# A decoder layer's output projection: attention rows in one tile pair, loaded in token halves by ScalarE, and the attention half first

## The chip, the cores and the metric

The kernel runs on one core of one Trainium2 chip. A core has a matrix engine (TensorE, in the profile PE, with its weight loads as PEld), three engines for elementwise work (VectorE or DVE, ScalarE or ACT, GpSimd or POOL), a synchronisation engine (SyncE or SP) that here only issues transfers, and 16 DMA engines that move data between DRAM and the core's own memory (SBUF) behind queues that SP, ACT and POOL feed. Each engine runs its own list of instructions in order and waits on semaphores where an operand or a buffer is not ready. The metric is device microseconds for one execution, the median of several. Before the change it is 1192.65 us (three runs, 1191.54 to 1194.22).

## The reference

One layer of a hybrid decoder over 1024 prompt tokens and 64 decode tokens (8 sequences of 8), model width 1024. Two mixers read one input projection: retention (8 heads of 64) and sliding-window attention (8 heads of 64). Their two results of 512 columns each are laid side by side and go through one output projection:

```python
h = x + jnp.concatenate([o_r, o_s], axis=-1) @ w_out     # 1088 x 1024 times 1024 x 1024
hf = rms_norm(h, norm_ffn_gain)
h = h + jnp.square(jax.nn.relu(hf @ w_up)) @ w_down      # 1024 -> 4096 -> 1024
```

`o_r` is the normalised and gated retention result, `o_s` the attention result. The change touches the first of these lines, and the buffers that the last one inherits from it. All is float32.

## The kernel before

**Arithmetic.** Every float32 operand is split into a rounded high part and a low remainder, and a product is three matmuls: high by high, low by high, high by low (`mm3`, lines 171 to 174; the profile shows them as L172, L173, L174, and L174 is the one that reads the low part of the moving operand). A split is `halve` (line 786): ACT casts the high part (L787), DVE or POOL subtracts to get the low part (L788). So each weight tile costs one ACT cast and one DVE subtraction before its first three matmuls can all run.

**Stages.** Input projection; sliding-window attention, whose results go as high and low parts to DRAM (`ms_hi_d`, `ms_lo_d`); retention in blocks t = 0 to 7 of 128 tokens and a decode block 8; the output projection; a product-saving two-level scheme for the MLP's up projection (`up`), which writes its activations to DRAM (`u_d`), and for its down projection, which reads them back (`ur`, split into `uh` and `ul`) and accumulates in the tiles `a`. The 1088 tokens are two groups s = 0, 1 of 544, each two halves h of 272: one matmul has 272 columns.

**Output projection.** It is transposed: for each m of 8 blocks of 128 output columns and each h, a PSUM tile `pso` gathers four k-steps of the retention half (weights `wor_m`, data `mixrh`, `mixrl`) and four of the attention half (`woa_m`, `mixah`, `mixal`): 24 matmuls. `wo_pair` (line 815) loads the raw weights of two m in one transfer on SP's queue (names ending in `_raw`) and splits them. `mix_load` (line 808) fetches the attention results of one s from DRAM, as one transfer of 1088 KB for the high and one for the low part, issued by SP (L811). The retention results come out of `mix_block`, in which ACT writes `mixrh` (L778) and POOL `mixrl` (L779). `residual` (line 831) fetches the residual input `y` by POOL's queue (L833), adds, stores it, and scales it for the MLP.

For s = 0 the projection (`out_early`) is interleaved with retention blocks 5, 6 and 7, two values of m behind each block, and m = 6, 7 behind the decode block. Its first values m = 0, 1 have the halves in the order retention, attention at h = 0 and attention, retention at h = 1. For s = 1 it runs alone after retention (`out_parts`), first the attention half of m = 0, 1, then the retention half.

**Memory.** Pools on the right side are placed one behind the other from the upper end of memory. At its upper end stands, up to the last `value_block`, the normalised input; the pools `mw` (weights `wa`, raw weights), `o`, `mxA` (attention rows of s = 1) and `mx0` (those of s = 0) take its place when the matmuls of `value_block` have read it. These are the matmuls `pst`. Later the pool `w` holds four weight tiles with the tag `wb`; in the MLP, weight tiles go to `wa` and `wb` in turn.

**What sets the order.** The program is written in the order above, and a planner, which simulates the engines, then sets each engine's list. So an edit can move instructions far from the place where it stands. The list of an engine is fixed when the kernel runs: an engine that waits for one instruction lets none behind it pass.

Of the kernel before, what the change touches and what calls it, by code (L numbers as in the profile page):

```python
# [20 lines left out]
P = 128  # L21
# [3 lines left out]
Q = 272  # L25
# [11 lines left out]
def hymba_layer(ctx: ExitStack, tc: tile.TileContext, a: dict, o: dict):  # L37
# [752 lines left out]
    def wsplit(src, tag, name, lo_eng):  # L790
        w = (mid if tag == "wb" else mw).tile([P, 2, 512], F32R, tag=tag, name=name, bufs=4)
        halve(w[:, 0, :], w[:, 1, :], src, lo_eng)
        return w
# [12 lines left out]
    mix, acc, fs, last_out = {}, {}, {}, [None]  # L806

    def mix_load(s, pl):
        for x, d_ in zip("hl", (ms_hi_d, ms_lo_d)):
            t_ = mix[s, "a" + x] = pl.tile([P, 4, 2, Q], F32R, tag="mixa" + x, name=f"mixa{x}{s}")  # L810
            nc.sync.dma_start(  # L811
                t_.bitcast(F32).rearrange("p k h n -> p k (h n)"), d_[:, :, 2 * Q * s : 2 * Q * s + 2 * Q]
            )
# [11 lines left out]
    def out_half(s, half, ps, h, w, first, last):  # L825
        for k in range(4):
            lh, ll = (w[:, i, k * 128 : k * 128 + 128] for i in range(2))
            mh, ml = (mix[s, half + x][:, k, h, :] for x in "hl")
            last_out[0] = mm3(ps, lh, ll, mh, ml, first and k == 0, last and k == 3)

    def residual(s, m, pss):
        y = om.tile([P, 2, Q], F32, tag="y", name=f"y{s}_{m}", bufs=2)
# [23 lines left out]
    def out_parts(s, ms, half, psum, pss):  # L856

        for m in ms:
            if m % 2 == 0:
                gen = wo_pair(s, m, half)  # L860
            w = next(gen)
            for h in range(2):
                if half == "a":
                    pss[m, h] = psum()
                out_half(s, half, pss[m, h], h, w, half == "a", half == "r")
# [89 lines left out]
    proj.close()  # L955
    mw = ctx.enter_context(pool("mw", side="right"))
# [5 lines left out]
    mxA = ox.enter_context(pool("mxA", side="right"))  # L962
    mx0x = ExitStack()
    mx0 = mx0x.enter_context(pool("mx0", side="right"))
    early = lambda: psA.tile([P, 512], F32, tag="mm", name="pso")[:, :Q]

    def out_early(m):

        if m and m % 2 == 0:
            gens["a"], gens["r"] = (wo_pair(0, m, x) for x in "ar")  # L970
            ahead.extend(next(gens[x]) for x in "ar")
        wa_, wr_ = ahead
        ahead.clear()
        if m % 2 == 0:
            ahead.extend(next(gens[x]) for x in "ar")
        pss = [early() for h in range(2)]
        for h in range(2):
            parts = [("a", wa_), ("r", wr_)]
            if m < 2 and h == 0:
                parts.reverse()  # L980
            for n, (half, w) in enumerate(parts):
                out_half(0, half, pss[h], h, w, n == 0, n == 1)
        residual(0, m, pss)()

    gens = {x: wo_pair(0, 0, x) for x in "ra"}
    ahead = [next(gens[x]) for x in "ra"][::-1]
    mix_load(0, mx0)
# [3 lines left out]
    for t in (5, 6, 7):  # L991
        mt = retention_block(t)
        for m in (2 * t - 10, 2 * t - 9):
            out_early(m)
        if t == 6:
            with tc.issue_after(last_load[0].ins):
                mix_load(1, mxA)
        mix_block(t, *mt)
    mix_block(8, *mt8)
    for m in (6, 7):  # L1000
        out_early(m)
# [52 lines left out]
    out_parts(1, (0, 1), "a", late, pss)  # L1054
# [6 lines left out]
    for ms in ((0, 1), (2, 3), (4, 5), (6, 7)):  # L1061
        if ms[0]:
            out_parts(1, ms, "a", late, pss)
        out_parts(1, ms, "r", late, pss)
# [20 lines left out]
    mid = ctx.enter_context(pool("w", side="right"))  # L1085
    ux = ExitStack()
# [304 lines left out]
```

## Time and profile before

| what | value |
|---|---|
| median of three runs | 1192.65 us (1191.54 to 1194.22) |
| the profiled execution, its own time | 1190.13 us |
| its span | 1188.3 us |
| mean granted TensorE clock in it | 0.998 |
| PE busy | 1173.1 us, 99% |
| DVE, ACT, POOL busy | 838.7 us, 513.6 us, 488.6 us (71%, 43%, 41%) |
| output projection's matmuls, first to last | 374.6 to 497.5 us in the span |

The span runs from the first to the last instruction of the profiled execution, and its own time lies 1.8 us above it. That execution lies 2.5 us below the median of the timed ones, so differences are to be formed inside one execution and then set against its own time or against the median, not mixed. In the rows of a timeline the columns are the start, the duration, the engine, the line, the operation and its tiles; in square brackets stands the idle time of the engine before the row, and what it waited for. Ends of matmuls are modelled: each is shown with about 0.29 us, while matmuls of 272 columns that follow one another start 0.125 us apart.

### The profile page before, as it was taken

How to read it: one execution, taken by the hardware profiler on the slowest of the kernel's cores; microseconds unless marked ns; L12 is line 12 of the kernel's file. 1: busy time of each engine (PE TensorE's matmuls, PEld its weight loads, DVE VectorE, ACT ScalarE, POOL GpSimd, SP SyncE). 2: the span in 40 equal slices, each digit the busy share in tenths (PEclk: the TensorE clock that was granted, in tenths of full speed). 3: DMA queues.
4: the chain of work that ended last, by engine and by line, in shares of the span. 5: the costliest groups of instructions: out<-in, count | busy, mean ns of one | idle time of the engine just before them, and what ended most of it. 6: DMA issues, size and time to landing. Idle time of an engine off the chain costs nothing.

```text
span 1188.3 us, 23487 instructions
## 1 busy us (share of the span) xinstructions
PE 1173.1 (99%) x9405; PEld 1126.8 (95%) x9405; DVE 838.7 (71%) x1546; ACT 513.6 (43%) x1055; POOL 488.6 (41%) x393
## 2 busy tenths in 40 slices
PE   9999999999999999999999999999999999999998
PEld 8999988989777999999999999999899999999998
DVE  7556768632356969887766677676788787888676
ACT  8343544553233437644444444444652333333231
POOL 0135333332434532466666666566472142053000
PEclk9999999999999999999999999999999999999999
DMA  7211234333326654343444434444684456443215
GB/s 246 73 62 68 92 102 169 101 116 103 99 72 229 210 165 155 116 156 124 149 152 148 146 128 142 149 148 158 246 278 149 153 171 201 143 163 97 76 59 187
DMA packets 102276, 169.44 MB, mean 143 GB/s; under 512 B 11999, under 2 KB 68255, under 8 KB 101911
## 3 DMA queue, kind: packets, MB, share of 16 engines
q1 hardware_dynamic: 87751, 122.68, 30.7%
q10 hardware_dynamic: 11856, 36.34, 9.4%
q0 software_dynamic: 2560, 8.91, 2.4%
q8 instruction: 74, 1.21, 0.4%
q14 instruction: 35, 0.29, 0.1%
HBM read 114.30 MB, written 53.61 MB: 141 GB/s over the span
## 4 chain that ended last, share of the span: by engine, by line
PE 83%; DVE 7%; issue 3%; DMA 2%; POOL 2%; ACT 2%; SPq 0%; ACTq 0%; DVEq 0%; POOLq 0%
PE psd L173 9%; PE psd L172 9%; PE psd L174 9%; PE psx L172 5%; PE psx L174 5%; PE psx L173 5%; PE psz L172 2%; PE psz L174 2%; PE psz L173 2%; PE pst L172 2%; PE pst L173 2%; PE pst L174 2%; PE psf L172 2%; PE psf L174 2%; PE psf L173 2%
## 5 line engine op out<-in xcount | busy, mean ns | idle before, releaser
L172 PE MATMUL psd<-uh,wd_w 128*128 128x272 f32 x896 | 259.1, 289 | 3.4 <-ACT a L1256 2.3
L173 PE MATMUL psd<-uh,wd_w 128*128 128x272 f32 x896 | 260.0, 290 | 0.0
L174 PE MATMUL psd<-ul,wd_w 128*128 128x272 f32 x896 | 258.5, 289 | 0.0
L172 PEld LDWEIGHTS psd<-uh,wd_w 128*128 128x128 f32 x896 | 169.8, 190 | 4.5 <-ACT a L1256 3.0
L174 PEld LDWEIGHTS psd<-ul,wd_w 128*128 128x128 f32 x896 | 169.4, 189 | 0.0
L173 PEld LDWEIGHTS psd<-uh,wd_w 128*128 128x128 f32 x896 | 169.1, 189 | 0.0
L1259 DVE TENSOR_TENSOR a<-a,psd 128x272 f32<-128x272 f32 x248 | 101.9, 431 | 50.4 <-PE psd L174 50.2
L788 DVE TENSOR_TENSOR wu_w<-wu_s,wu_w 128x512 fp32r<-128x512 f32 x64 | 59.7, 937 | 50.4 <-ACT wu_w L787 49.7
L787 ACT CAST wd_w<-wd_s 128x512 fp32r<-128x512 f32 x64 | 37.4, 623 | 115.8 <-PE psd L174 104.0
L788 DVE TENSOR_TENSOR ul<-ur,uh 128x1088 fp32r<-128x1088 f32 x56 | 81.8, 1487 | 2.8 <-ACT uh L787 2.8
L1113 DVE SCALAR_TENSOR_TENSOR m<-m,rsf 128x272 f32<-128x272 f32 x96 | 74.6, 777 | 3.2 <-ACT rsf L910 0.5
L172 PE MATMUL psx<-op_1h,wu_w 128*128 128x272 f32 x256 | 74.3, 290 | 0.4 <-ACT m L1129 0.4
L174 PE MATMUL psx<-op_1l,wu_w 128*128 128x272 f32 x256 | 74.1, 289 | 0.0
L172 PE MATMUL psx<-op_0h,wu_w 128*128 128x272 f32 x256 | 74.1, 290 | 0.0
L174 PE MATMUL psx<-op_0l,wu_w 128*128 128x272 f32 x256 | 74.1, 289 | 0.0
L173 PE MATMUL psx<-op_1h,wu_w 128*128 128x272 f32 x256 | 73.7, 288 | 0.0
L173 PE MATMUL psx<-op_0h,wu_w 128*128 128x272 f32 x256 | 73.7, 288 | 0.0
L362 POOL TENSOR_TENSOR sp<-sp,ssp 128x1024 f32<-128x1024 f32 (+1 forms) x16 | 28.6, 1789 | 88.4 <-DVE ssp L361 60.0
L172 PE MATMUL psf<-hnh,wqk_hi 128*128 128x384 f32 (+1 forms) x192 | 63.5, 331 | 0.2 <-DVE qkst L514 0.2
L787 ACT CAST uh<-ur 128x1088 fp32r<-128x1088 f32 x56 | 59.6, 1101 | 9.5 <-PE psd L173 9.1
L174 PE MATMUL psf<-hnl,wqk_hi 128*128 128x384 f32 (+1 forms) x192 | 63.2, 329 | 0.0
L173 PE MATMUL psf<-hnh,wqk_lo 128*128 128x384 f32 (+1 forms) x192 | 62.8, 327 | 0.0
(342 smaller groups left out, 3618.7 us busy)
## 6 DMA issues: line engine op xcount, KB each, us to landing
ur<-u_d SPq DMA_DIRECT2D x51, 544.0 KB, 5.0
u_d<-r4t SPq DMA_DIRECT2D x32, 544.0 KB, 4.5
wu_r<-in_w_up ACTq DMA_DIRECT2D x32, 512.0 KB, 4.4
wd_r<-in_w_down ACTq DMA_DIRECT2D x30, 512.0 KB, 6.6
u_d<-r3t SPq DMA_DIRECT2D x32, 408.0 KB, 2.7
y<-in_xY POOLq DMA_DIRECT2D x16, 272.0 KB, 3.2
y_d<-y POOLq DMA_DIRECT2D x16, 272.0 KB, 2.9
yt<-y_d SPq DMA_DIRECT2D x16, 272.0 KB, 2.8
```

Of the source, the lines that this page charges most:

```text
L172: nc.tensor.matmul(ps, lh, rh, start=first, stop=False, skip_group_check=more)
L173: nc.tensor.matmul(ps, ll, rh, start=False, stop=False, skip_group_check=more)
L174: return nc.tensor.matmul(ps, lh, rl, start=False, stop=last, skip_group_check=more)
L362: nc.gpsimd.tensor_tensor(s, s, ss.unsqueeze(2).broadcast_to([P, 4, n]), ALU.mult)
L787: nc.scalar.copy(hi, src)
L788: lo_eng.tensor_tensor(lo, src, hi.bitcast(F32), ALU.subtract)
L1113: nc.vector.scalar_tensor_tensor(t_, src, 0.0, rsf[:, s, h, :], ALU.max, ALU.mult)
L1259: added[i] = nc.vector.tensor_tensor(to, to, ps, ALU.add).ins
```

## The change

The attention rows of both s lie in one tile pair in a pool of its own, `mxw`, opened first on the right side, that is at the upper end of memory. `mix_load` fills it in four transfers of 544 KB, token half by token half; for s = 0 ACT issues them, for s = 1 SP does after the last matmuls of s = 0. In every step of s = 0 the attention half comes first; m = 6 and 7 are done together, all attention parts and then all retention parts. For s = 1 the first values m = 0, 1 begin with the retention half. The `y` tiles of s = 0 have four buffers, in `mx0`. PSUM tiles of s = 0 beyond the third come from a second pool. When the output projection has ended, the attention tiles are reused as the four `wb` weight tiles.

```diff
     def wsplit(src, tag, name, lo_eng):
-        w = (mid if tag == "wb" else mw).tile([P, 2, 512], F32R, tag=tag, name=name, bufs=4)
+        if tag == "wb":
+            w = wbs[wbn[0] % 4]
+            wbn[0] += 1
+        else:
+            w = mw.tile([P, 2, 512], F32R, tag=tag, name=name, bufs=4)
         halve(w[:, 0, :], w[:, 1, :], src, lo_eng)
...
-    def mix_load(s, pl):
-        for x, d_ in zip("hl", (ms_hi_d, ms_lo_d)):
-            t_ = mix[s, "a" + x] = pl.tile([P, 4, 2, Q], F32R, tag="mixa" + x, name=f"mixa{x}{s}")
-            nc.sync.dma_start(
-                t_.bitcast(F32).rearrange("p k h n -> p k (h n)"), d_[:, :, 2 * Q * s : 2 * Q * s + 2 * Q]
-            )
+    def mix_load(s, eng):
+        for x in "hl":
+            mix[s, "a" + x] = mxw.tile([P, 4, 2, Q], F32R, tag="mixa" + x, name=f"mixa{x}{s}")
+        for h in range(2):
+            c0 = Q * (2 * s + h)
+            for x, d_ in zip("hl", (ms_hi_d, ms_lo_d)):
+                eng.dma_start(mix[s, "a" + x].bitcast(F32)[:, :, h, :], d_[:, :, c0 : c0 + Q])
...
-        y = om.tile([P, 2, Q], F32, tag="y", name=f"y{s}_{m}", bufs=2)
+        y = (om if s else mx0).tile([P, 2, Q], F32, tag="y", name=f"y{s}_{m}", bufs=2 if s else 4)
...
     proj.close()
+    mxw = ctx.enter_context(pool("mxw", side="right"))
     mw = ctx.enter_context(pool("mw", side="right"))
...
-    mxA = ox.enter_context(pool("mxA", side="right"))
...
-    early = lambda: psA.tile([P, 512], F32, tag="mm", name="pso")[:, :Q]
...
+    def early(n):
+        pl, tag, bufs = (psA, "mm", 3) if n < 3 else (psB, "t1", 2)
+        return pl.tile([P, 512], F32, tag=tag, name="pso", bufs=bufs)[:, :Q]
...
-        for h in range(2):
-            parts = [("a", wa_), ("r", wr_)]
-            if m < 2 and h == 0:
-                parts.reverse()
-            for n, (half, w) in enumerate(parts):
-                out_half(0, half, pss[h], h, w, n == 0, n == 1)
-        residual(0, m, pss)()
...
+        parts = [(m, h, x) for m in ms for h in range(2) for x in "ar"]
+        if len(ms) == 2:
+            parts.sort(key=lambda p_: p_[2])
+        for m, h, x in parts:
+            if x == "a":
+                pss[m, h] = early(len(pss))
+            out_half(0, x, pss[m, h], h, ws[m, x], x == "a", x == "r")
+        for m in ms:
+            residual(0, m, [pss[m, h] for h in range(2)])()
 
-    gens = {x: wo_pair(0, 0, x) for x in "ra"}
-    ahead = [next(gens[x]) for x in "ra"][::-1]
-    mix_load(0, mx0)
+    mix_load(0, nc.scalar)
+    gens = {x: wo_pair(0, 0, x) for x in "ar"}
+    ahead = [next(gens[x]) for x in "ar"]
...
-            out_early(m)
-        if t == 6:
-            with tc.issue_after(last_load[0].ins):
-                mix_load(1, mxA)
+            out_early((m,))
         mix_block(t, *mt)
     mix_block(8, *mt8)
-    for m in (6, 7):
-        out_early(m)
+    out_early((6, 7))
+    mix_load(1, nc.sync)
...
-    out_parts(1, (0, 1), "a", late, pss)
+    out_parts(1, (0, 1), "r", late, pss)
...
     for ms in ((0, 1), (2, 3), (4, 5), (6, 7)):
+        out_parts(1, ms, "a", late, pss)
         if ms[0]:
-            out_parts(1, ms, "a", late, pss)
-        out_parts(1, ms, "r", late, pss)
+            out_parts(1, ms, "r", late, pss)
...
     mid = ctx.enter_context(pool("w", side="right"))
+    for x in "hl":
+        t_ = mxw.tile([P, 4, 2, Q], F32R, tag="mixa" + x, name="wb" + x).rearrange("p k h n -> p (k h n)")
+        wbs.extend(t_[:, i : i + 1024].rearrange("p (j n) -> p j n", j=2) for i in (0, 1024))
```

The planner's lists change at the places below. In them `woa_0` is the attention half's weight tile for m = 0, `wor_0` the retention half's; `state` is the retention state that DVE updates with the PSUM tile `pur`; `orrr` the head norm of a retention block and `mtr` its normalised result, which PE then transposes into `pm`.

VectorE, where the output projection begins, behind the last product `rptr` of retention block 5, before:

```order
L713 TENSOR_TENSOR rptr_4115<-rsr_4108,intra 128x512
L788 TENSOR_TENSOR wor_0_4218<-wor_0_raw,wor_0_4218 128x512
L749 SCALAR_TENSOR_TENSOR state_3387<-state_3386,decs,pur_4027 64x64 x8
L612 TENSOR_REDUCE orrr_4047<-osqr_4045 128x8
L788 TENSOR_TENSOR woa_0_4223<-woa_0_raw,woa_0_4223 128x512
L788 TENSOR_TENSOR woa_1_4328<-woa_0_raw,woa_1_4328 128x512
L788 TENSOR_TENSOR wor_1_4331<-wor_0_raw,wor_1_4331 128x512
L613 TENSOR_SCALAR orrr_4047<-orrr_4047 128x8
L615 TENSOR_TENSOR mtr_4044<-ror_4004,orrr_4047 128x512
```

And with the change:

```order
L713 TENSOR_TENSOR rptr_4115<-rsr_4108,intra 128x512
L749 SCALAR_TENSOR_TENSOR state_3387<-state_3386,decs,pur_4027 64x64 x8
L612 TENSOR_REDUCE orrr_4047<-osqr_4045 128x8
L788 TENSOR_TENSOR woa_0_4224<-woa_0_raw,woa_0_4224 128x512
L613 TENSOR_SCALAR orrr_4047<-orrr_4047 128x8
L788 TENSOR_TENSOR wor_0_4229<-wor_0_raw,wor_0_4229 128x512
L788 TENSOR_TENSOR woa_1_4330<-woa_0_raw,woa_1_4330 128x512
L788 TENSOR_TENSOR wor_1_4333<-wor_0_raw,wor_1_4333 128x512
L615 TENSOR_TENSOR mtr_4044<-ror_4004,orrr_4047 128x512
```

The first low part that PE's list asks for stood ahead of the eight state updates (`wor_0`) and now stands behind them and behind the reduction of `orrr` (`woa_0`); the short `orrr` step L613 stands two subtractions earlier.

TensorE at the same place, first rows behind `pur`, before (twelve matmuls of `wor_0` stand first, and then four of `woa_0`):

```order
L737 MATMUL pur_4027<-vtr_3606,kdr_4002 64x64 x8
L172 MATMUL pso<-mixrh,wor_0_4218 128x272
L173 MATMUL pso<-mixrh,wor_0_4218 128x272
L174 MATMUL pso<-mixrl,wor_0_4218 128x272
L172 MATMUL pso<-mixrh,wor_0_4218 128x272
```

With the change (twelve of `woa_0`, and then twelve of `wor_0`):

```order
L737 MATMUL pur_4027<-vtr_3606,kdr_4002 64x64 x8
L172 MATMUL pso<-mixah_4216,woa_0_4224 128x272
L173 MATMUL pso<-mixah_4216,woa_0_4224 128x272
L174 MATMUL pso<-mixal_4217,woa_0_4224 128x272
L172 MATMUL pso<-mixah_4216,woa_0_4224 128x272
```

Before, 30 matmuls of `pso` stand between `pur` and the transposes `pm`; with the change 32 of them and two matmuls `rsr` of the next block's scores.

ScalarE, where the down projection begins (`ur` are activations read back from DRAM, `uh_74` their high parts, `wd_r` raw down weights that ACT's queue loads, `a` the accumulators that ACT copies from PSUM), before:

```order
L1114 ACTIVATE r_1_10070<-m_1_9917 128x272
L1214 DMA ur_74_10084<-u_d_131 128x4x272 x2
L1214 DMA ur_5_10087<-u_d_131 128x4x272
L1256 COPY a_10093<-psd 128x272 x8
L787 CAST wd_w_10242<-wd_s_10240 128x512
L787 CAST wd_w_10307<-rw_6_9947 128x512
L787 CAST wd_w_10369<-wd_s_10168 128x512
L787 CAST wd_w_10372<-wd_s_9952 128x512
L802 DMA wd_r_10586<-in_w_down 128x1024
L787 CAST uh_74_10085<-ur_74_10084 128x1088
L802 DMA wd_r_10588<-in_w_down 128x1024
L1256 COPY a_10178<-psd 128x272
```

And with the change (the lines of the changed kernel are numbered 12 higher here; `wbh` and `wbl` are the reused tiles):

```order
L787 CAST wbl<-rw_6_9905 128x512
L1126 ACTIVATE r_1_10027<-m_1_9876 128x272
L1226 DMA ur_74_10041<-u_d_131 128x4x272 x2
L1226 DMA ur_5_10044<-u_d_131 128x4x272
L1268 COPY a_10050<-psd 128x272 x8
L787 CAST wbl<-wd_s_10195 128x512
L787 CAST wd_w_10322<-wd_s_10124 128x512
L787 CAST wbh<-wd_s_9910 128x512
L806 DMA wd_r_10536<-in_w_down 128x1024
L806 DMA wd_r_10538<-in_w_down 128x1024
L787 CAST uh_74_10042<-ur_74_10041 128x1088
L1268 COPY a_10133<-psd 128x272
```

The cast of `uh_74` stood ahead of the second `wd_r` transfer and now stands behind it, between it and the copy `a`; the cast of `rw_6` moved ahead of `r_1`.

More of the change, by code (lines that the diff above doesn't have):

```diff
@@ L803, in rawload @@
         return raw
-    mix, acc, fs, last_out = {}, {}, {}, [None]
-    def mix_load(s, pl):
-        for x, d_ in zip("hl", (ms_hi_d, ms_lo_d)):
-            t_ = mix[s, "a" + x] = pl.tile([P, 4, 2, Q], F32R, tag="mixa" + x, name=f"mixa{x}{s}")
-            nc.sync.dma_start(
-                t_.bitcast(F32).rearrange("p k h n -> p k (h n)"), d_[:, :, 2 * Q * s : 2 * Q * s + 2 * Q]
-            )
+    mix, acc, fs, last_out, wbs, wbn = {}, {}, {}, [None], [], [0]
+    def mix_load(s, eng):
[5 more added lines that the diff above has]
+                eng.dma_start(mix[s, "a" + x].bitcast(F32)[:, :, h, :], d_[:, :, c0 : c0 + Q])
     def wo_pair(s, m, half):
@@ L862, in out_parts @@
             for h in range(2):
-                if half == "a":
+                fresh = (m, h) not in pss
+                if fresh:
                     pss[m, h] = psum()
-                out_half(s, half, pss[m, h], h, w, half == "a", half == "r")
+                out_half(s, half, pss[m, h], h, w, fresh, not fresh)
     def operands(s, m):
@@ L961, in hymba_layer, with out_early @@
         mix[1, "r" + x] = om.tile([P, 4, 2, Q], F32R, tag="mixr" + x, name="mixr1" + x)
-    mxA = ox.enter_context(pool("mxA", side="right"))
     mx0x = ExitStack()
     mx0 = mx0x.enter_context(pool("mx0", side="right"))
-    early = lambda: psA.tile([P, 512], F32, tag="mm", name="pso")[:, :Q]
-    def out_early(m):
-        if m and m % 2 == 0:
-            gens["a"], gens["r"] = (wo_pair(0, m, x) for x in "ar")
-            ahead.extend(next(gens[x]) for x in "ar")
[L972 to L976, printed above, removed]
-        for h in range(2):
-            parts = [("a", wa_), ("r", wr_)]
-            if m < 2 and h == 0:
-                parts.reverse()
-            for n, (half, w) in enumerate(parts):
-                out_half(0, half, pss[h], h, w, n == 0, n == 1)
-        residual(0, m, pss)()
-    gens = {x: wo_pair(0, 0, x) for x in "ra"}
-    ahead = [next(gens[x]) for x in "ra"][::-1]
-    mix_load(0, mx0)
+    def early(n):
+        pl, tag, bufs = (psA, "mm", 3) if n < 3 else (psB, "t1", 2)
+        return pl.tile([P, 512], F32, tag=tag, name="pso", bufs=bufs)[:, :Q]
+    def out_early(ms):
+        if ms[0] % 2 == 0 and ms[0]:
+            gens["a"], gens["r"] = (wo_pair(0, ms[0], x) for x in "ar")
+            ahead.extend(next(gens[x]) for x in "ar")
+        ws, pss = {}, {}
+        for m in ms:
+            ws[m, "a"], ws[m, "r"] = ahead
+            ahead.clear()
+            if m % 2 == 0:
+                ahead.extend(next(gens[x]) for x in "ar")
+        parts = [(m, h, x) for m in ms for h in range(2) for x in "ar"]
[5 more added lines that the diff above has]
+            out_half(0, x, pss[m, h], h, ws[m, x], x == "a", x == "r")
+        for m in ms:
+            residual(0, m, [pss[m, h] for h in range(2)])()
+    mix_load(0, nc.scalar)
+    gens = {x: wo_pair(0, 0, x) for x in "ar"}
+    ahead = [next(gens[x]) for x in "ar"]
     mix_block(4, *held[4])
```

## The prediction

> **What bounds the kernel now.** I read the page first, then the groups of waits of TensorE, then the timelines of all engines where the lists change.
>
> ```profile
> span 1188.3 us, 23487 instructions
> PE 1173.1 (99%) x9405; PEld 1126.8 (95%) x9405; DVE 838.7 (71%) x1546; ACT 513.6 (43%) x1055; POOL 488.6 (41%) x393
> PE psd L172 <- ACT a L1256: 2.3, 3, 1.7
> PE pm L767 <- DVE mtr L615: 0.7, 1, 0.7
> PE pso L172 <- DMA mixah<-ms_hi_d: 0.6, 1, 0.6
> PE pso L173 <- DVE woa L788: 0.5, 1, 0.5
> PE pso L173 <- DVE wor L788: 0.4, 1, 0.4
> ```
>
> PE is the bound: 1173.1 of 1188.3 us. The change takes no matmul away, so it can act only through PE's idle time and its clock. The last five rows (us in total, times, longest) are what this change can reach: four waits of the output projection, 2.2 us together, and one place at the start of the down projection, 2.3 us. Nothing larger can be won there. The projection begins like this on PE:
>
> ```profile
> 373.97 0.69 PE L737 MATMUL pur<-vtr,kdr 128*64 128x64 f32 x16
> 375.13 0.29 PE L172 MATMUL pso<-mixrh,wor 128*128 128x272 f32 x1
> 375.25 0.29 PE L173 MATMUL pso<-mixrh,wor 128*128 128x272 f32 x1
> 377.03 0.36 PE L172 MATMUL pso<-mixah,woa 128*128 128x272 f32 x1 [0.61 <-DMA mixah<-ms_hi_d]
> 377.86 0.39 PE L173 MATMUL pso<-mixah,woa 128*128 128x272 f32 x1 [0.47 <-DVE woa L788]
> 379.06 0.39 PE L173 MATMUL pso<-mixrh,wor 128*128 128x272 f32 x1 [0.44 <-DVE wor L788]
> 381.70 0.52 PE L767 MATMUL pm<-c_ident,mtr 128*128 128x128 f32 x3 [0.75 <-DVE mtr L615]
> ```
>
> The matmuls of `wor_0` fill the time from 374.66 until the attention rows land, and every wait is short. A packed matmul costs 0.125 us (375.13 to 375.25). What feeds it on VectorE:
>
> ```profile
> 373.37 1.35 DVE L788 TENSOR_TENSOR wor<-wor_raw,wor 128x512 fp32r<-128x512 f32 x1
> 374.70 1.78 DVE L749 SCALAR_TENSOR_TENSOR state<-state,decs,pur 64x64 f32<-64x64 f32 x8
> 376.52 0.69 DVE L612 TENSOR_REDUCE orrr<-osqr 128x8 f32<-128x512 f32 x1
> 377.12 1.28 DVE L788 TENSOR_TENSOR woa<-woa_raw,woa 128x512 fp32r<-128x512 f32 x2
> 378.92 0.17 DVE L613 TENSOR_SCALAR orrr<-orrr 128x8 f32<-128x8 f32 x1
> 380.86 0.69 DVE L615 TENSOR_TENSOR mtr<-ror,orrr 128x512 f32<-128x512 f32 x1 [1.78 <-POOL orrr L614]
> ```
>
> **The entry, step by step.** With the change PE's first group needs `woa_0`, whose low part stands on DVE behind the eight state updates and the reduction. The updates need `pur`, which PE ends at 374.66, so they begin where they begin now and the low part is ready at about 377.12 + 0.64 = 377.8. Until then PE can run one matmul (high by high); the matmuls of `wor_0`, which filled this time, stand behind. So four short waits are traded for one of about 3.1 us, 374.66 to 377.85. From there 31 matmuls of `pso` and two of `rsr` stand ahead of `pm`, 33 x 0.125 = 4.1 us, so PE reaches `pm` at 381.95. `mtr` is then ready: L613 moves up to 377.8, POOL's power follows to 379.8 (1.8 us, the wait in the last row), DVE meanwhile runs three subtractions of 0.64 us, `mtr` ends at about 380.6. Before, `pm` started at 381.70 with 30 + 0 of these matmuls behind PE, now with 32 + 2: four more, 0.5 us of work. Net 381.95 - 0.5 - 381.70 = -0.25 us.
>
> Against this stands the load of the attention rows:
>
> ```profile
> 370.80 0.53 SPq L811 DMA_DIRECT2D mixah<-ms_hi_d  x1
> 371.03 0.69 ACT L593 ACTIVATE vtr<-pst,rst 128x512 f32<-128x512 f32 x1 [4.84 <-PE pst L174]
> 371.07 1.33 POOL L833 DMA_DIRECT2D y<-in_xY  x2 [6.82 <-PE pst L174]
> mixah<-ms_hi_d SPq DMA_DIRECT2D x2, 1088.0 KB, 7.1
> mixal<-ms_lo_d SPq DMA_DIRECT2D x2, 1088.0 KB, 9.8
> y<-in_xY POOLq DMA_DIRECT2D x16, 272.0 KB, 3.2
> 374.53:377.94 3.41, 2.33 (x20) 1.88 (x14) 3.35 (x12) 1.75 (x4) 1.34 (x1) 1.00 1.04 401
> ```
>
> ACT issues the four transfers behind `vtr`, from about 371.8, one us later than SP did. The first halves of high and low rows are together 1088 KB, what `mixah` alone was (issued at 370.80, awaited until 377.0, so 6.1 us): estimate 378.0 for the low rows of h = 0, needed by the third matmul at 378.1. But POOL now issues six `y` loads there instead of two, 1088 KB more, while the DMA share is already 1.04 in 374.53 to 377.94 at 401 GB/s (last two columns): at most 2.7 us at that rate, if all of them came first. I take 0.25 us, because SP's other loads were in that share before too, and so 0.0 us for the entry; ends -0.3 (no DMA wait) and +2.4. ACT's four issues (0.5 to 0.6 us each as on SP) push `osqr` at most 1.2 us, to about 375.3, still ahead of DVE's reduction at 376.5: nothing.
>
> **The clock.** What does a wait of 3 us cost beyond itself? Three windows (us, then busy time of PE, PEld, DVE, ACT, POOL, granted clock, DMA share, GB/s):
>
> ```profile
> 852.40:855.81 3.41, 1.41 (x10) 0.97 (x9) 0.93 (x2) 1.84 (x5) 0.00 (x0) 1.00 1.02 414
> 855.81:859.22 3.41, 3.41 (x16) 3.41 (x17) 2.75 (x3) 3.41 (x9) 0.14 (x1) 0.50 0.89 311
> 859.22:862.63 3.41, 3.41 (x29) 3.41 (x29) 1.69 (x2) 2.69 (x9) 3.33 (x3) 1.00 1.02 359
> ```
>
> After a stretch with PE busy for 1.41 of 3.41 us the clock was 0.50 for one stretch, in which 16 matmuls started instead of 29: 13/29 x 3.41 = 1.5 us lost. The entry as it is now (2.33 of 3.41 in the window quoted above) did not cause this. With a wait of 3.1 us one such stretch there has at most half of its time busy, wherever its border falls, and when most of the wait lies in one stretch, less than 1.41. So I count a halved stretch at the entry: +1.5 us; ends 0 and 1.5.
>
> The Trainium skill (TensorE: Matmul & The Clock Gate, "What's actually happening") says that the clock falls back after at least one idle window of about 3.4 us, on a free-running count. Read strictly, neither 2.0 us idle at 852.40 nor 3.1 us here would do it; the trace disagrees, with 1.41 us of work inside the window that preceded the half clock. By the skill's rule this term would be 0 and the result 1193.9.
>
> **The start of the down projection.** ScalarE, VectorE and PE:
>
> ```profile
> 850.24 1.17 ACT L787 CAST uh<-ur 128x1088 fp32r<-128x1088 f32 x1
> 853.59 0.34 ACTq L802 DMA_DIRECT2D wd_r<-in_w_down  x1
> 853.97 0.39 ACT L1256 COPY a<-psd 128x272 f32<-128x272 f32 x1 [2.56 <-DMA u_d<-r4t]
> 854.25 1.11 ACT L787 CAST uh<-ur 128x1088 fp32r<-128x1088 f32 x1
> 851.62 1.28 DVE L788 TENSOR_TENSOR ul<-ur,uh 128x1088 fp32r<-128x1088 f32 x1
> 854.41 0.39 PE L172 MATMUL psd<-uh,wd_w 128*128 128x272 f32 x1 [1.74 <-ACT a L1256]
> 855.69 0.51 PE L172 MATMUL psd<-uh,wd_w 128*128 128x272 f32 x1 [0.27 <-ACT a L1256]
> ```
>
> The `wd_r` transfer at 853.59 waits for a store (`u_d<-r4t`), and behind it stands the copy `a` that frees PE's bank. The first cast of `uh_74` (1.17 us) is done in the shade of this wait now; with the change it stands behind it. So the copy comes at 853.97 + 1.11 = 855.1, PE goes on at 855.5 with two matmuls, and its third needs the low part, 855.1 + 1.28 = 856.4. The second cast and the next copies follow on ACT, so PE's second group starts at about 856.95 instead of 855.69: +1.26. Bounds: 0, if the halved stretch that follows now falls elsewhere and takes back 1.5; +2.8, if a second stretch is halved. I take +1.2. The cast of `rw_6` ahead of `r_1` costs at most its own 0.7 us on ACT there, 7 us earlier; it lies inside the same wait, since PE's resumption hangs on the store: nothing.
>
> **Edits at nothing.** The attention rows of s = 1 are now issued when PE has ended the last attention half of s = 0, about 441 us. PE then has the retention halves of m = 6, 7 and the first group of s = 1, 96 matmuls x 0.125 = 12 us, and the longest load of such rows took 10.3 us (`mixal`, the second issue); cover gone, 1 to 2 us. Four `y` buffers: PE never waited for `y`. The `wb` tiles turn over by fours as before, and their splits are on DVE and ACT, busy 71% and 43%. I give all of these 0, with 0.5 to both sides.
>
> **Sum.** 0.0 + 1.5 + 1.2 = +2.7 us. The profiled execution (1190.13 us, 1.8 us above its span) would go to 1192.8; it lies 2.5 us below the median of the runs, on which I put the same difference: 1192.65 + 2.7 = 1195.3 us.
>
> **Rivals.** *No halved stretch at the entry*: the border falls so that each side keeps enough work, or the threshold lies lower than 1.41 us. For it: the trace has a single case. Then 1192.65 + 1.2 = 1193.9. (The rule of the Trainium skill's page TensorE: Matmul & The Clock Gate, cited above, leads to the same.) *Faster*: the waits vanish as the new order suggests, because the attention rows land earlier and PE loses none of its 2.2 us; and the halved stretch at 855.81 falls away (-1.5) since its border lies elsewhere. Then 1192.65 - 2.2 - 1.5 = 1189.0, or 1190.5 with the waits alone. Against it: DVE's list puts `woa_0` behind the state updates, and nothing ends `pur` earlier. *The loads collide*: six `y` loads, the weights and the attention halves share the 16 engines, the low rows of h = 0 land 2.4 us late and the high rows of h = 1 behind them; decided when they land after 378.1. Then 1195.3 + 2.4 = 1197.7. *The planned order of the down projection does not matter*, because the store ends earlier than now (before 852.5, when PE runs dry): then only the entry counts, 1194.2.
>
> **Chances.** The forecast 0.40, no halved stretch 0.25, faster 0.15, collision 0.12, down projection without effect 0.08. About 0.2%, 2.4 us, is what a measurement of this kernel can tell from no change: 1190.3 to 1195.0 is no change. The forecast lies just beyond its edge, so of its 0.40 I give 0.28 to slower; with the collision 0.12 and some of the others 0.42 slower. Faster 0.14 from its case, the rest, 0.44, no change. The range, 1190.4 to 1198.2, leaves out the far ends of the faster case and of the collision; the forecast's own is 1193.5 to 1196.8.
>
> **What would show it.** In the changed profile: PE with one wait of about 3 us between `pur` and the second matmul of `woa_0`, ended by DVE, and no wait for `mtr`; a stretch of 3.41 us at half clock between 378 and 385; at the start of the down projection a wait of about 2.8 us for the copy and one of about 0.6 us for `ul`. It would be wrong if the first matmuls of `woa_0` started before 377, if the clock stayed at 1.00 behind the wait, or if `mixal` ended the wait after 379.

## The result and the profile after

The change makes the kernel slower: 1198.63 us (median of six runs, 1195.84 to 1200.14) against 1191.01 us for the kernel before in the same comparison (six runs, 1189.49 to 1194.22). The ratio is 1.0055, with a 95% interval of 1.0042 to 1.0068: 6.6 us, between 5.0 and 8.1. The direction is that of the prediction's sum, though its chances stood almost level (0.42 for slower, 0.44 for no change). The size was not forecast: +2.7 us was predicted, and the measured median lies 0.4 us above the upper end of the range; set on the base that the prediction used, 1192.65 + 6.6 = 1199.2 us, it lies 1.0 us above. Two single executions of experiment kernels, at 1575.72 us (a_late_dn) and 2286.94 us (a_late_dn2), are left out of the ratios below.

The profiled execution took 1195.84 us, 5.7 us more than the one of before, and like that one it lies near the fast end of its kernel's runs. First the page and the waits of TensorE (us in total, times, longest us):

```profile
span 1193.8 us, 23495 instructions
PE 1171.7 (98%) x9405; PEld 1126.5 (94%) x9405; DVE 840.0 (70%) x1546; ACT 513.5 (43%) x1055; POOL 494.0 (41%) x393
PE pso L174 <- DMA mixal<-ms_lo_d: 3.2, 1, 3.2
PE psd L172 <- ACT a L1268: 3.1, 2, 1.6
PE pso L173 <- DVE woa L788: 1.4, 1, 1.4
PE pso L172 <- DMA mixah<-ms_hi_d: 1.4, 1, 1.4
```

PE does the same work and idles 22.1 us instead of 15.2 (span less busy time), 6.9 us more. The timeline of PE where the projection begins:

```profile
373.57 0.69 PE L737 MATMUL pur<-vtr,kdr 128*64 128x64 f32 x16
375.67 0.36 PE L172 MATMUL pso<-mixah,woa 128*128 128x272 f32 x1 [1.41 <-DMA mixah<-ms_hi_d]
377.46 0.39 PE L173 MATMUL pso<-mixah,woa 128*128 128x272 f32 x1 [1.43 <-DVE woa L788]
381.03 0.59 PE L174 MATMUL pso<-mixal,woa 128*128 128x272 f32 x1 [3.18 <-DMA mixal<-ms_lo_d]
387.21 0.60 PE L767 MATMUL pm<-c_ident,mtr 128*128 128x128 f32 x4
```

From `pur` to `pm` it is 13.6 us instead of 7.7, of which four more matmuls are 0.5 us. That is the whole difference of the profile: from `pm` to the projection's last matmul it takes 115.8 us in both, and the up projection, from its first matmul to the first of the down projection, takes 336.2 us in both. The stretches of 3.41 us at the entry (PE busy, PEld, DVE, ACT, POOL, granted clock, DMA share, GB/s):

```profile
375.42:378.83 3.41, 0.76 (x2) 0.37 (x2) 3.38 (x10) 0.98 (x2) 1.99 (x2) 1.00 1.06 364
378.83:382.24 3.41, 1.21 (x5) 1.21 (x6) 1.14 (x2) 0.62 (x1) 0.79 (x2) 0.50 1.07 357
382.24:385.66 3.42, 3.42 (x17) 3.42 (x16) 0.00 (x0) 0.00 (x0) 1.26 (x1) 0.50 1.11 353
```

The clock is at half for two stretches, and the share of the DMA engines is above 1 throughout. The loads of the attention rows, as ACT issued them, and their median time to landing:

```profile
370.63 0.69 ACT L593 ACTIVATE vtr<-pst,rst 128x512 f32<-128x512 f32 x1 [4.87 <-PE pst L174]
370.64 0.59 ACTq L818 DMA_DIRECT2D mixah<-ms_hi_d  x1
371.27 0.63 ACTq L818 DMA_DIRECT2D mixal<-ms_lo_d  x1
mixah<-ms_hi_d ACTq DMA_DIRECT2D x2, 544.0 KB, 8.6
mixal<-ms_lo_d ACTq DMA_DIRECT2D x2, 544.0 KB, 12.3
```

The first low half is awaited until 381.03 - 371.27 = 9.8 us after its issue, as long as the whole tile of twice its size took before in the median. And at the start of the down projection:

```profile
853.22 0.39 PE L172 MATMUL psd<-uh,wd_w 128*128 128x272 f32 x1 [1.62 <-ACT a L1268]
860.96 0.40 PE L172 MATMUL psd<-uh,wd_w 128*128 128x272 f32 x1 [1.46 <-ACT a L1268]
862.00 0.39 PE L174 MATMUL psd<-ul,wd_w 128*128 128x272 f32 x1 [0.52 <-DVE ul L788]
848.87 0.92 DVE L788 TENSOR_TENSOR wbl<-rw,wbl 128x512 fp32r<-128x512 f32 x1
849.71 1.01 DVE L1125 SCALAR_TENSOR_TENSOR m<-m,rsf 128x272 f32<-128x272 f32 x1
```

The first of these waits was shorter in the kernel before:

```profile
846.36 0.39 PE L172 MATMUL psd<-uh,wd_w 128*128 128x272 f32 x1 [0.33 <-ACT a L1256]
```

In this execution no halved stretch follows, which takes the added waits back; the down projection lasts 350.5 us, and 350.4 before. The other runs show a mean clock of 0.992 to 0.994 where this one has 0.997, and one halved stretch takes 0.5 x 3.41 / 1194 = 0.0014 off this mean, so they had some two to four of them more.

### The profile page after: what moved, and what is told of

Its sections match the earlier page's. It is cut to its first block, busy times and chain, and to the rows that moved or that the text cites. A ratio compares the mean times of both kernels' runs of the same rounds, so it can differ in the third digit from the quotient of the medians.

```text
span 1193.8 us, 23495 instructions
## 1 busy us (share of the span) xinstructions
PE 1171.7 (98%) x9405; PEld 1126.5 (94%) x9405; DVE 840.0 (70%) x1546; ACT 513.5 (43%) x1055; POOL 494.0 (41%) x393
## 4 chain that ended last, share of the span: by engine, by line
PE 87%; DVE 6%; DMA 2%; POOL 2%; issue 1%; ACT 1%; SPq 0%; ACTq 0%; POOLq 0%; DVEq 0%
PE psd L174 9%; PE psd L173 9%; PE psd L172 9%; PE psx L172 5%; PE psx L174 5%; PE psx L173 5%; PE psz L173 3%; PE psz L174 2%; PE psz L172 2%; PE pso L172 2%; PE pso L174 2%; PE pso L173 2%; PE pst L172 2%; PE pst L173 2%; PE pst L174 2%; PE psf L172 2%
## 5 line engine op out<-in xcount | busy, mean ns | idle before, releaser
L172 PE MATMUL psd<-uh,wd_w 128*128 128x272 f32 x448 | 129.7, 290 | 5.1 <-ACT a L1268 3.1
L174 PE MATMUL psd<-ul,wd_w 128*128 128x272 f32 x448 | 129.3, 289 | 0.5 <-DVE ul L788 0.5
L173 PE MATMUL psd<-uh,wd_w 128*128 128x272 f32 x448 | 128.2, 286 | 0.0
L172 PEld LDWEIGHTS psd<-uh,wd_w 128*128 128x128 f32 x448 | 84.5, 189 | 6.3 <-ACT a L1268 3.5
L173 PEld LDWEIGHTS psd<-uh,wd_w 128*128 128x128 f32 x448 | 84.9, 190 | 0.0
L174 PEld LDWEIGHTS psd<-ul,wd_w 128*128 128x128 f32 x448 | 84.2, 188 | 0.7 <-DVE ul L788 0.7
L787 ACT CAST wd_w<-wd_s 128x512 fp32r<-128x512 f32 x32 | 19.9, 623 | 114.3 <-PE psd L174 104.8
L173 PE MATMUL psd<-uh,wbl 128*128 128x272 f32 x224 | 65.2, 291 | 0.0
L173 PE MATMUL psd<-uh,wbh 128*128 128x272 f32 x224 | 65.2, 291 | 0.0
L174 PE MATMUL psd<-ul,wbh 128*128 128x272 f32 x224 | 64.6, 288 | 0.0
L174 PE MATMUL psd<-ul,wbl 128*128 128x272 f32 x224 | 64.6, 288 | 0.0
L172 PE MATMUL psd<-uh,wbl 128*128 128x272 f32 x224 | 64.2, 287 | 0.0
L172 PE MATMUL psd<-uh,wbh 128*128 128x272 f32 x224 | 64.2, 287 | 0.0
L1173 POOL TENSOR_TENSOR r4t<-r3t,r4t 128x272 f32<-128x272 f32 x60 | 61.0, 1027 | 1.3
```

Of the source, the lines that this page charges most:

```text
L172: nc.tensor.matmul(ps, lh, rh, start=first, stop=False, skip_group_check=more)
L173: nc.tensor.matmul(ps, ll, rh, start=False, stop=False, skip_group_check=more)
L174: return nc.tensor.matmul(ps, lh, rl, start=False, stop=last, skip_group_check=more)
L787: nc.scalar.copy(hi, src)
L1173: sub = lambda o_, p_, q_: eng.tensor_tensor(o_, p_, q_, ALU.subtract)
```

## The experiments

Twelve kernels were run in three groups; each ratio is to the kernel before in the same group (1191.15 to 1191.4 us; for the change 1191.01).

| kernel | ratio, 95% interval | us against before | `pur` to the last `pso`, us | clock halved at the entry |
|---|---|---|---|---|
| before | 1 | 0 | 123.5 | no |
| the change | 1.0055 (1.0042 to 1.0068) | +6.6 | 129.4 | yes |
| a_y2 | 1.0047 (1.0031 to 1.0064) | +5.6 | 127.1 | yes |
| a_rfirst | 1.0059 (1.0044 to 1.0074) | +7.0 | 128.6 | yes |
| b_afirst | 1.0031 (1.0018 to 1.0044) | +3.7 | 127.9 | yes |
| a_sync | 1.0008 (0.9996 to 1.0021) | +1.0 | 127.3 | yes |
| a_fill | 1.0062 (1.0044 to 1.0079) | +7.4 | 128.9 | no |
| a_late | 1.0021 (1.0011 to 1.0031) | +2.5 | 126.4 | yes |
| a_late_dn | 1.0016 (1.0006 to 1.0027) | +1.9 | 126.7 | yes |
| a_late_dn2 | 1.0015 (1.0002 to 1.0029) | +1.8 | 126.2 | yes |
| a_lf8 | 1.0012 (1.0001 to 1.0022) | +1.4 | 125.0 | no |
| a_late_y2 | 1.0002 (0.9992 to 1.0012) | +0.2 | 123.4 | no |
| a_wbfix | 1.0037 (1.0023 to 1.0051) | +4.4 | 129.2 | yes |
| b_dn | 1.0000 (0.9991 to 1.0010) | 0.0 | 124.2 | no |

The fourth column comes from one profile each (start of `pur` to start of the last matmul of `pso`), the last from the granted clock in its windows.

### First group: loads or order?

**a_y2: two `y` loads at the entry instead of six.**

```diff
-        y = (om if s else mx0).tile([P, 2, Q], F32, tag="y", name=f"y{s}_{m}", bufs=2 if s else 4)
+        y = om.tile([P, 2, Q], F32, tag="y", name=f"y{s}_{m}", bufs=2)
```

> The changed kernel with the y tiles of s = 0 back in the old pool with two buffers, so two y loads instead of six stand at the entry (1088 KB less). Theory (the loads collide): at the 370 GB/s that the changed kernel's trace shows there, 1088 KB are 2.9 us; the low attention rows of h = 0 land about 378 instead of 381.0, PE's wait for mixal falls from 3.2 to below 0.5 us, and with less idle time in one piece at most one halved stretch of the clock follows instead of two; time 3 to 5 us below the changed kernel, still 1 to 3 us above the kernel before. Rival (the order alone, attention first, is the loss): the wait only changes its name, time within 1 us of the changed kernel.

The wait for `mixal` is gone, as the theory of colliding loads said, and the stage is 2.3 us shorter in the profile; but only about 1 us of time came back by the ratios, within the intervals (2.9 us by the medians, of four runs). PE still waited 1.49 us for `mixah` and 1.35 us for `woa_0`, and then worked at half clock:

```profile
379.58 0.36 PE L172 MATMUL pso<-mixah,woa 128*128 128x272 f32 x1 [1.49 <-DMA mixah<-ms_hi_d]
381.30 0.59 PE L173 MATMUL pso<-mixah,woa 128*128 128x272 f32 x1 [1.35 <-DVE woa L788]
383.40:386.80 3.40, 3.40 (x17) 3.40 (x16) 0.69 (x1) 0.01 (x1) 1.31 (x2) 0.50 1.11 347
```

So the `y` loads do delay the rows (the median time to landing of the low halves falls from 12.3 to 8.8 us), but they are not enough of the cause.

**a_rfirst: the retention half first again.**

```diff
+        elif ms[0] < 2:
+            parts[0], parts[1] = parts[1], parts[0]
         for m, h, x in parts:
-            if x == "a":
+            fresh = (m, h) not in pss
+            if fresh:
                 pss[m, h] = early(len(pss))
-            out_half(0, x, pss[m, h], h, ws[m, x], x == "a", x == "r")
+            out_half(0, x, pss[m, h], h, ws[m, x], fresh, not fresh)
...
-    gens = {x: wo_pair(0, 0, x) for x in "ar"}
-    ahead = [next(gens[x]) for x in "ar"]
+    gens = {x: wo_pair(0, 0, x) for x in "ra"}
+    ahead = [next(gens[x]) for x in "ra"][::-1]
```

> The changed kernel with the retention half first again in h = 0 of m = 0 and 1, everything else kept. Rival (the order alone is the loss): 5 us or more come back, time as the kernel before. Theory (the loads collide, and ACT's four issues have moved the weight casts behind the head norm): PE still waits for the first low weight part, behind the state updates, about 2.8 us in one piece, and then for mixal about 1.7 us; 1.5 to 2.5 us come back, time 4 to 5 us above the kernel before.

Nothing came back, so the order of the halves alone is not the loss; the theory's 1.5 to 2.5 us were a miss too. PE now waits for the same split under another name (2.17 us for `wor`, whose low part the planner again puts behind the state updates), and the rows are late behind it.

**b_afirst: the kernel before, attention half first.**

```diff
-            if m < 2 and h == 0:
-                parts.reverse()
...
-    gens = {x: wo_pair(0, 0, x) for x in "ra"}
-    ahead = [next(gens[x]) for x in "ra"][::-1]
+    gens = {x: wo_pair(0, 0, x) for x in "ar"}
+    ahead = [next(gens[x]) for x in "ar"]
```

> The kernel before with the attention half first in m = 0 and 1, everything else kept (whole tiles loaded by SP, two y loads). Theory (loads): high rows land at 377 as before and low rows at 381, and the list lets PE run only six matmuls until the transposes pm at 381.7, so PE idles about 5 us there without the y loads: 2 to 4 us above the kernel before, plus 1.5 us for a halved stretch. Rival (order does not matter, only the y loads do): within 1 us of the kernel before.

As the theory said, 3.7 us slower than the kernel before. With the rows landing at 376.6, attention first leaves PE with nothing to do, and a list of six matmuls ahead of `pm`:

```profile
PE pm L767 <- DVE mtr L615: 2.8, 1, 2.8
PE pso L172 <- DMA mixah<-ms_hi_d: 2.4, 1, 2.4
```

**a_sync: the transfers on SP's queue.**

```diff
-    mix_load(0, nc.scalar)
+    mix_load(0, nc.sync)
```

> The changed kernel with the four transfers of s = 0 issued by SP instead of ACT. Its list then has them ahead of the first weights of the projection. Theory (loads): the rows land early, about 375 to 379, but the raw weights come behind them and the low part of woa_0 later, about 380; PE does the next block's transposes and products meanwhile; time 1 to 4 us below the changed kernel. Rival (the order alone): no gain over the changed kernel, within 1 us of it.

5.6 us came back, more than expected, and the trace shows something that neither theory had:

```profile
362.00 0.62 SPq L818 DMA_DIRECT2D mixah<-ms_hi_d  x1
364.02 0.76 SPq L818 DMA_DIRECT2D mixal<-ms_lo_d  x1
```

SP issues the first and the last of the four from 362.0 to 364.8. The new place at the upper end of memory is free 8.6 us earlier than ACT used it: ACT's list has the transfers behind `vtr`, and `vtr` waits for the last matmul of `value_block` until 370.6. PE's list also changes here (it goes on with the next block while it waits for the weights, whose loads now stand behind the rows), so this run doesn't separate the two.

### Second group: the loads early, and the clock

**a_fill: 44 idle matmuls in the wait.**

```diff
             if x == "a":
                 pss[m, h] = early(len(pss))
+            if (m, h, x) == (0, 0, "a"):
+                f = mix[0, "rh"][:, 0, 0, :]
+                for _ in range(44):
+                    nc.tensor.matmul(pss[m, h], f[:, :128], f, start=True, stop=True)
```

> The changed kernel with 44 matmuls of 272 columns without use (retention rows times themselves, into the bank that the first group then overwrites) between pur and the first matmul of woa_0; no other row of any engine's list moves. They take 44 x 0.125 = 5.5 us and lie inside the 6.0 us for which PE stood idle there. Theory (the halved clock costs beside the waits): the clock stays at 1.00 from 378 to 386, in which the changed kernel ran at 0.50 from 381.0 to 385.7, and 2.1 us come back: 4.5 us above the kernel before instead of 6.6. Rival (the clock does not follow from idleness, or costs nothing): no difference, or the fillers' own time on top.

The clock stays at 1.00, and no time comes back (+7.4 us, 5.2 to 9.4). The rows say why:

```profile
377.39 0.69 PE L737 MATMUL pur<-vtr,kdr 128*64 128x64 f32 x16
378.01 5.84 PE L996 MATMUL pso<-mixrh 128*128 128x272 f32 x44
385.00 0.39 PE L174 MATMUL pso<-mixal,woa 128*128 128x272 f32 x1 [0.91 <-DMA mixal<-ms_lo_d]
389.78 0.39 PE L172 MATMUL pso<-mixah,woa 128*128 128x272 f32 x1 [1.51 <-DMA mixah<-ms_hi_d]
391.52 0.60 PE L767 MATMUL pm<-c_ident,mtr 128*128 128x128 f32 x4
```

At full clock PE reaches the second half of the rows before it has landed and waits there. `pm` comes 14.1 us after `pur` began, and 13.6 us in the changed kernel with its halved clock. So one more thing did move, other than the expectation says: in the trace five more matmuls of `pso` stand ahead of `pm` than in the changed kernel, 5 x 0.125 = 0.6 us. In the changed kernel the slow clock lies on top of a wait that is there anyway.

**a_late: SP issues the rows, behind the first weights.**

```diff
-    mix_load(0, nc.scalar)
     gens = {x: wo_pair(0, 0, x) for x in "ar"}
     ahead = [next(gens[x]) for x in "ar"]
+    mix_load(0, nc.sync)
```

> The changed kernel with the four transfers of s = 0 issued by SP, behind the first raw weights of the projection instead of ahead of them; PE's list at the entry begins as in the changed kernel (12 of woa_0, 12 of wor_0). Theory (the place in the queue: on ACT the transfers stand behind vtr, which waits for PE until 370.6, while the memory at the upper end is free from 362.0): the rows land before 373, the low part of woa_0 stands ahead of the state updates again, none of the five waits at the entry is left, no halved stretch there; the projection ends 2 us earlier than in the kernel before, and what stays is the start of the down projection: 2 us below to 1 us above the kernel before. Rival (the order attention first costs by itself): 3 us or more above the kernel before, as b_afirst.

4.1 us come back; no wait for the rows is left. It is not the gain that was expected, since PE still waits 2.2 us for the low part of `woa_0`, 0.9 us for that of `wor_0`, and the clock is halved:

```profile
376.57 0.39 PE L173 MATMUL pso<-mixah,woa 128*128 128x272 f32 x1 [2.19 <-DVE woa L788]
379.58 0.60 PE L173 MATMUL pso<-mixrh,wor 128*128 128x272 f32 x1 [0.89 <-DVE wor L788]
372.78 3.74 DVE L788 TENSOR_TENSOR woa<-woa_raw,woa 128x512 fp32r<-128x512 f32 x1
370.72 2.71 POOL L838 DMA_DIRECT2D y<-in_xY  x5 [2.20 <-PE pst L174]
373.45 1.29 POOL L779 TENSOR_TENSOR mixrl<-gt,mixrh 128x512 fp32r<-128x512 f32 x1
374.69 1.27 POOL L728 TENSOR_TENSOR qdr<-qt,qdec 128x512 f32<-128x512 f32 x1
374.38:377.79 3.41, 1.23 (x10) 1.22 (x10) 3.38 (x8) 1.31 (x3) 1.58 (x2) 1.00 1.07 374
```

The subtraction, which stands ahead of the state updates in DVE's list again, took 3.74 us instead of 0.68: it ends 0.6 us after POOL's second operation does. The rows were issued at 362.4 to 364.9, by another queue and some 8 us earlier than in the changed kernel; no run changes only one of the two.

**a_late_dn and a_late_dn2: the second `wd_r` transfer behind the first cast of `uh_74`, or behind the eight copies.**

```diff
-        nc.scalar.dma_start(raw, src)
+        with tc.issue_after(cast74[0].ins) if name == "wd2_r2" else ExitStack():
+            nc.scalar.dma_start(raw, src)
...
```

This comes on top of the edit of a_late; the lines that fill `cast74`, the first cast of `uh_74`, are left out here; a_late_dn2 has `copied[6]`, the last of the copies, in its place.

> a_late with one row of ACT's list moved back: the second wd_r transfer behind the first cast of uh_74, as in the kernel before. Theory (prediction's term for the down projection, +1.2 us): 1.0 to 1.3 us below a_late. Rival (PE's wait there is set by the store and the clock, not by the cast): no difference to a_late.

> a_late with that one transfer behind all eight copies a of the block, so that neither cast nor copy waits for the store. Theory: the whole wait at the start of the down projection (1.5 to 1.7 us, and 0.5 us for ul behind it) goes, with no halved stretch after it: 2 to 3 us below a_late, 2 to 4 us below the kernel before. Rival (something else is late next, the banks by DVE or the weights): 0 to 1 us below a_late.

0.6 and 0.7 us below a_late, with intervals that overlap its own: half of what was expected of the first, and a third or less of what was expected of the second. Nothing clear came of either: both lie where the rivals put them.

### Third group: each rest by itself

**a_lf8: a_late with eight idle matmuls.** The edit is that of a_fill with `range(8)`.

> a_late with 8 matmuls of 272 columns without use between pur and the first matmul of woa_0; no other row of any list moves. In a_late PE waits 2.2 us there for the low part of woa_0, and 0.9 us later for that of wor_0, and the clock is at 0.50 from 377.5 to 384.4. The fillers take 1.0 us of the wait away without delaying anything. Theory (a halved clock costs where PE has work and nothing else is late): the clock stays at 1.00 and 2 us come back against a_late, 0.5 us above the kernel before. Rival (as in a_fill, something else is late there): no difference to a_late.

The clock stays at 1.00 through the entry, and 1.1 us come back by the ratios (1.8 by the medians). The two intervals overlap, so the times alone do not show it; in the profiles the stage is 1.4 us shorter, with the eight idle matmuls in it. Here, where no load is late, the halved clock appears to cost; the sign is as expected, the size somewhat less.

**a_late_y2: a_late with two `y` loads.** The edit is that of a_y2.

> a_late with the y tiles of s = 0 back in the old pool with two buffers. In a_late the subtraction for woa_0 took 3.74 us on DVE instead of 0.68, from 372.8, while POOL issued the y loads until 373.4 and then ran two operations until 376.0, back to back. Theory (DVE's subtraction of two operands from memory stands while POOL works, and gets its turn in a gap): with two y loads POOL is through 2.5 us earlier, the subtraction takes 1.3 us as in the kernel before, PE's wait for it falls from 2.2 to 0.6 us; 1 to 2.5 us below a_late. Rival (the subtraction waited for its data): it stays above 3 us and the time within 0.5 us of a_late.

```profile
373.94 0.56 POOL L838 DMA_DIRECT2D y<-in_xY  x1 [4.37 <-PE pst L174]
375.53 1.27 POOL L779 TENSOR_TENSOR mixrl<-gt,mixrh 128x512 fp32r<-128x512 f32 x1 [1.03 <-DMA mixah<-ms_hi_d]
376.00 1.35 DVE L788 TENSOR_TENSOR woa<-woa_raw,woa 128x512 fp32r<-128x512 f32 x1
380.48 0.39 PE L173 MATMUL pso<-mixrh,wor 128*128 128x272 f32 x1 [1.29 <-DVE wor L788]
384.32 0.63 PE L767 MATMUL pm<-c_ident,mtr 128*128 128x128 f32 x4 [1.31 <-DVE mtr L615]
```

The subtraction takes 1.35 us, the wait for it is gone, the clock is not halved, and the kernel is level with the one before (+0.2 us, -1.0 to +1.4). With rows on SP's queue in good time and two `y` loads, the changed kernel's attention first costs nothing.

**a_wbfix: the changed kernel with the down projection's start as before.**

```diff
-                behind = act_load.ins if (g, i) == (0, 5) else copied[DOWN[f] if g == 1 else 4] if g in (1, 2) and i == 1 else None
+                behind = act_load.ins if (g, i) == (0, 5) or (g, i, f) == (0, 4, 1) else copied[DOWN[f] if g == 1 else 4] if g in (1, 2) and i == 1 else None
```

and the edit of a_late_dn.

> The changed kernel with ACT's and DVE's lists at the start of the down projection as in the kernel before: the split of rw_6 behind the loads of ur, and the second wd_r transfer behind the first cast of uh_74; the entry of the output projection is untouched. Theory (both moved rows cost: PE's first wait there was 1.62 us in the changed kernel and 0.33 in the kernel before, and 0.5 us more for ul): 1.5 to 2.5 us below the changed kernel. Rival (the clock decides, or the store is late next): within 0.7 us of the changed kernel.

```profile
852.89 0.39 PE L172 MATMUL psd<-uh,wd_w 128*128 128x272 f32 x1 [0.46 <-ACT a L1273]
860.86 0.39 PE L172 MATMUL psd<-uh,wd_w 128*128 128x272 f32 x1 [1.70 <-ACT a L1273]
862.15 0.40 PE L172 MATMUL psd<-uh,wd_w 128*128 128x272 f32 x1 [0.27 <-ACT a L1273]
```

The waits are those of the kernel before again, and the kernel is 2.1 us faster than the changed one by the ratios, as expected, though the two intervals overlap. If so, both rows that moved there cost together about what the theory said; the row of `rw_6` was the larger part in the profile (the first wait falls from 1.62 to 0.46 us).

**b_dn: the kernel before, without copies and casts behind the store.**

```diff
-        nc.scalar.dma_start(raw, src)
+        with tc.issue_after(copied[6]) if name == "wd2_r2" else ExitStack():
+            nc.scalar.dma_start(raw, src)
```

> The kernel before with one row of ACT's list moved: the second wd_r transfer behind the eight copies a of the block, so that neither the copies nor the casts of uh stand behind the store it waits for. Theory (this wait, 1.7 us, and the halved stretch behind it, 1.5 us, go): 1.5 to 3 us below the kernel before, faster than both. Rival (the activations read back, ur, land late next, as for the second group of a_late_dn2): 0 to 0.7 us below the kernel before.

No gain (0.9991 to 1.0010): the rival. What was late next is the activations read back:

```profile
856.31 1.10 ACT L787 CAST uh<-ur 128x1088 fp32r<-128x1088 f32 x1 [2.09 <-DMA ur<-u_d]
857.75 0.39 PE L172 MATMUL psd<-uh,wd_w 128*128 128x272 f32 x1 [1.56 <-ACT a L1257]
```

PE's wait of 1.74 us moved by one block and became 1.56. No kernel tried is faster than the kernel before.

## Why the prediction was right or wrong

**What bounds, and where.** Right: PE is the bound, its work is unchanged, and the loss lies at the two places named.

**The entry's first wait.** Right in its end and its cause: PE ran one matmul and then waited until the low part of `woa_0`, behind the state updates, at 377.46 (377.85 predicted, and everything started 0.4 us earlier). It came in two pieces, though: 1.41 us for the high rows, until 375.67, and 1.43 us for the low part. The wait for `mtr` is gone, as predicted.

**The landing of the low rows: the step that failed.** The prediction put `mixal` at 378.0 and took 0.25 us for the six `y` loads, up to 2.4 at the far end. PE waited 3.18 us, until 381.03: past 379, which the prediction itself had named as a sign of being wrong. The transfers even went out earlier than it assumed (the first at 370.64, not 371.8), so the low rows were there 10.4 us after the first issue, where the sum had 6.1. That figure was carried over from 1088 KB that SP issued ahead of its other loads, with two `y` loads beside them; on ACT's queue the rows shared the DMA engines, whose busy share was above 1, with SP's `kt` and weights and POOL's six `y` loads. In its place the runs show: with the loads early on SP's queue this wait is gone (a_late), and with two `y` loads it is gone as well (a_y2). The Trainium skill (DMA: Bandwidth & Descriptors, "Queues, rings and completion order") says that each DMA engine takes the queues that have work in turn, a packet at a time; the landings here agree with it (9.8 us for the half tile on a third queue), though no run isolated that rule. The rival of colliding loads, given 0.12, named the mechanism; its price was too low: 1.5 + 2.4 = 3.9 us for the entry, where from `pur` to `pm` it cost 5.9.

**The clock.** Predicted: a halved stretch at the entry, +1.5 us. It came, twice as long, and the trace's rule (busy 1.41 of 3.41 us halves the clock) held again with 0.76 and, in a_late, 1.23 of 3.41. The rule of the Trainium skill (TensorE: Matmul & The Clock Gate, "What's actually happening"), a whole idle window of about 3.4 us, read strictly would have left the clock alone here, where PE's longest gap was 3.18 us; these rows do not bear it out. One step of the working was loose: a border in the middle of a wait of 3.1 us leaves up to 1.86 of 3.41 us busy on each side, a little more than half, and a_lf8 kept its clock with 1.77. But the term did not add: a_fill shows that with the clock kept, PE only waits for the next late load. Where loads are in time it seems to cost, 1.1 to 1.8 us for two stretches (a_late against a_lf8, intervals that overlap). That is why undoing the `y` loads alone (a_y2) or the slow clock alone (a_fill) gave little, early rows gave most (a_late, 4.1 of 6.6 us), and early rows with two `y` loads gave all (a_late_y2).

**The start of the down projection.** The cast of `uh_74`, +1.2 us: the waits came in the order described (1.46 us, 2.8 foretold, and 0.52 us for `ul`), but together they are as long as before (1.46 + 0.52 against 1.74 + 0.27 us), and moving the row back gave 0.6 us, too little to tell from nothing or from 1.2. The row of `rw_6` was put at nothing, on the ground that PE's resumption hangs on the store behind it. That was wrong: its DVE half (0.92 us) went ahead of the scaling of `m`, so `r`, three load issues of 1.9 us and the copies came later, and PE's first wait, which has nothing to do with the store, rose from 0.33 to 1.62 us. All these waits together grew by 1.26 us, the very size foretold, but from the row put at nothing: that was luck. Both rows together are worth 2.1 us by a_wbfix's ratio, with intervals that overlap.

**Edits at nothing.** Right for the rows of s = 1 (no wait of PE for them) and for the `wb` tiles' turnover in the loop (336.2 us for the up projection in both). The four `y` buffers were judged by PE's waits for `y` and cost through their loads instead.

**What stays open.** a_late changes the rows' queue, the time of their issue and the place of the subtraction in DVE's list together, and which of these counts most is not separated. a_late_y2 has the changed start of the down projection, which a_wbfix puts at 2.1 us, and yet is only 0.2 us slower than the kernel before; the intervals allow that, but its entry isn't seen to be faster. And the halved stretches outside the entry fall elsewhere from run to run (the mean clock of one kernel's runs spans 0.994 to 1.0), so differences of less than 1 us are not read here.

## What to carry to other kernels

A load goes out when its place in an engine's list comes, not when its memory is free: before moving a load to another engine, look at what stands ahead of it there. The time to landing of a row belongs to the queue and the traffic it was measured in; where the share of the DMA engines is already 1, count all bytes issued in the same microseconds, of all queues. And where several causes of idleness overlap (late loads, a slow clock, a late split), undoing one can show little: undo them together, then one by one.

## What the hardware showed that was not expected

A subtraction of two operands from memory on VectorE (0.68 us alone) took 3.74 us while POOL finished issuing loads and ran two operations back to back (a_late), and 1.35 us when it got its turn between them (a_late_y2). The Trainium skill (SBUF — State Buffer, "SBUF: two separate sides") describes this: the two engines share a pair of ports that the first to start holds for its whole instruction while the other stands. The rows agree that one stands while the other works; that the first to start holds the ports they do not show, for in a_late the subtraction started at 372.78, ahead of POOL's first operation (373.45), while POOL still issued `y` loads, and stood through both. a_late against a_late_y2 puts this standing, with the clock that it halves and the four loads themselves, at 2.3 us.

A halved clock came back only after a stretch in which PE was busy almost throughout (least 3.14 of 3.41 us, in a_rfirst). In a_late, a stretch at half clock with 2.53 of 3.42 us busy was followed by another halved one, while at full clock 2.33 of 3.41 (kernel before) did no harm:

```profile
377.79:381.21 3.42, 2.53 (x12) 2.21 (x11) 2.99 (x8) 0.62 (x1) 0.32 (x1) 0.50 0.50 180
381.21:384.62 3.41, 3.41 (x17) 3.41 (x17) 1.04 (x2) 0.00 (x0) 2.59 (x2) 0.50 0.91 271
384.62:388.03 3.41, 3.41 (x53) 3.17 (x52) 1.29 (x2) 0.78 (x2) 1.39 (x2) 1.00 0.81 252
```

And how little work keeps the clock: in a_lf8 a stretch at the entry with 1.77 of 3.41 us busy was followed by full clock, and one at the start of the down projection with 1.47 by half clock (the borders at the entry are counted back from the change of the clock at 852.73 in steps of 3.41 us):

```profile
378.27:381.68 3.41, 1.77 (x12) 1.55 (x12) 3.35 (x11) 0.21 (x1) 0.49 (x1) 1.00 1.04 375
849.32:852.73 3.41, 1.47 (x12) 1.24 (x11) 2.85 (x4) 1.58 (x6) 3.33 (x4) 1.00 0.43 121
```

At the entry of a_y2 a stretch with 1.73 us busy (376.73 to 380.14) was still followed by half clock.

Before the output projection this reading fails. In five profiles (a_y2, a_fill, a_late_dn2, a_lf8, a_late_y2) a stretch at 318 to 324 us counted as 2.6 us busy, with seven to nine matmuls in it, was followed by a halved one, while the changed kernel kept its clock after a stretch there with the same busy time and 17 matmuls; and in a_rfirst one at 304.33 to 307.74 us that counts as busy throughout was followed by a halved one. So the busy time of the rows isn't all that the clock goes by. That stage was not looked into.
